# The split of transposed probabilities in two attention mixers, with and without the scheduler's priority

## The chip, the cores and the metric

The kernel runs on one core of a Trainium2 chip. The metric is the device time of one execution in microseconds (us); lower is better. Engines are named as in the profile: PE is TensorE, with PEld for its weight loads, DVE is VectorE, ACT is ScalarE, POOL is GpSimd and SP is SyncE.

## What is computed

Two layers of a bidirectional encoder run over 768 tokens (a prompt of 512 and a sample of 256) with a model width of 1024. Each layer is a half feed-forward block, a mixer, and a second half feed-forward block. The mixer of layer 0 joins a chunked spatial gating with a windowed attention with sinks; that of layer 1 is a neighbourhood attention on a grid.

```python
def even_layer(x, ...):
    x = x + 0.5 * swiglu(rmsnorm(x, f1_n), f1_g, f1_u, f1_d)
    x = x + mixer_ab(rmsnorm(x, mix_n), w_in, sgu_ln_g, sgu_ln_b, sgu_w, sgu_b, sink, w_out)
    x = x + 0.5 * swiglu(rmsnorm(x, f2_n), f2_g, f2_u, f2_d)

def mixer_ab(h, ...):
    z = h @ w_in
    zs = gelu(z[..., :1024]); u, vh = zs[..., :512], layer_norm(zs[..., 512:])
    vmix = einsum('gij,bnjgc->bnigc', sgu_w, vh) + sgu_b      # chunks of 128 tokens, 4 groups
    a_out = u * vmix
    b_out = window_gqa(rope_partial(q), rope_partial(k), v, sink)   # 8 heads, 2 of keys and values
    return concatenate([a_out, b_out]) @ w_out

def window_gqa(q, k, v, sink):
    s = (q @ k^T over blocks n-1, n, n+1 of 128 tokens) * 64 ** -0.5, masked to |distance| <= 128
    p = softmax(concatenate([s, sink]))[..., :-1]
    return p @ v

def mixer_c(h, w_qkv, rpb, w_out):
    q, k, v = h @ w_qkv                                        # 16 heads of 64
    return neighbourhood_attn(q, k, v, rpb) @ w_out            # window 8 x 16 on a grid 64 wide, with bias
```

## The kernel before

Activations lie channel-major: 1024 channels are eight tiles of 128 partitions, and the 768 tokens lie along the free axis in groups of 512 and 256. A product in fp32 is made of three products of halves: every operand is split into a high part, a cast made on ACT (L122 for weights, whi; L208 for data), and a low part, which DVE subtracts (L123, wlo; L209, with the names tl, vhl, ol and others). Weights come in blocks of 512 KB through SP's queue. PSUM is held in two pools, `mm` for projections (ps_mm) and `aux` for the rest (ps_aux), with four banks of 128x512 each; the next tile of a pool waits for the last reader of the bank that it takes over.

The order of PE's instructions is written by hand: generators are started with delays on a planned time, and each product lets those whose time has come emit theirs. The context around the whole build (L1767) fixes that order for PE alone. On the other engines a list scheduler places the instructions, each when its operands are expected and by a priority that follows the order in the code; `tc.high_priority()` lets what is emitted inside it go ahead of other ready work on its engine. It stands in a few places already, such as the norms.

Mixer 0 runs from about 545 to 715 us of the span. Its attention goes through 12 pairs of a key head and a block of queries. `score` makes the scores of four heads into aux banks, and `finish_rows` the softmax in place: maximum (L1097), its negative (L1101), four exponentials on ACT (L1103), the sink's part (L1107 to L1109), the reciprocal (L1111) and four scalings p (L1113). `turn` (L1222 on) transposes up to three blocks of p by PE into an aux bank each (L156) and splits each bank into th and tl, of which there are three buffers. `values` multiplies both by the values and adds the two halves of the result, through a copy tb on ACT (L1242) and additions on DVE (L1248).

Beside it run the projections of the queries, with their rotation (`roped`, L1153 to L1156: a shuffle ru and a product rt from the projection's bank, a product on ru, the sum), and then the high and low part of q (L1374). `stats` gets the gating input's mean and scale (mv, up to L1304), ACT applies them (L1310, vg), the split follows (vhh on ACT, vhl on DVE), PE mixes them with the gating weights (swh, swl), and L1319 adds the bias into the output tiles o. `u_part` projects the other half (L1350), applies the gelu on ACT (L1351) and multiplies it in (L1354).

Mixer 1 runs from about 1755 to 2065 us. Its attention works on pairs of heads; `split_t` (L1458 on) transposes four blocks of probabilities into one aux bank and splits it into th and tl. Beside it run the projections of q, k and v (qk at L1577, vt at L1594).

Of the kernel before, what the change touches and what calls it, by code (L numbers as in the profile page):

```python
# [55 lines left out]
class Trunk:  # L56
# [1061 lines left out]
    def mixer0(self):  # L1118
# [104 lines left out]
        def turn(kv, n, blks, p):  # L1223
            res = []
            for i, b in enumerate(blks):
                pt = self.psum(self.aux, "aux")
                for r in range(4):
                    self.tpose(pt[:, r * P : (r + 1) * P], p[r][:, i * P : (i + 1) * P])
                th = mp.tile([P, 512], F32R, tag="th", name="th", bufs=3)
                tl = mp.tile([P, 512], F32R, tag="tl", name="tl", bufs=3)  # L1230
                self.split(th, tl, pt)
                res.append((th, tl))
            return res

# [21 lines left out]
        def attention(gap):  # L1256
            cur = None
            for kv in (0, 1):
                for n in range(6):
                    while len(qheads) < 2 * kv + 2:  # L1260
                        yield 0.5
                    new = score(kv, qheads[2 * kv : 2 * kv + 2], n)
                    scored.append((kv, n))
                    yield gap
                    if cur:
                        values(*cur[:3], tt)
                        valued.append(cur[:2])
                    yield gap
                    cur = new
                    tt = turn(*cur)  # L1270
                    yield 0.3 * gap
            yield 1.0
            values(*cur[:3], tt)
# [125 lines left out]
    def mixer1(self):  # L1399
# [57 lines left out]
        def split_t(src):  # L1457
            pt = self.psum(self.aux, "aux")  # L1458
            for i, s in enumerate(src):
                self.tpose(pt[:, i * P : (i + 1) * P], s)  # L1460
            th = mp.tile([P, 512], F32R, tag="th", name="th", bufs=3)
            tl = mp.tile([P, 512], F32R, tag="tl", name="tl", bufs=3)
            self.split(th, tl, pt)
            return th, tl

        def put(h, po, c0, c1):
# [32 lines left out]
        def prompt(pr, p, vt, hv):  # L1499

            while len(vt) < 6:
                yield 0.5
            for h in (0, 1):
                a, b, c, d = p[0][h] + p[1][h]
                tt = []
                for src in ((a[:, lo], d[:, hi], a[:, hi], b[:, lo]), (b[:, hi], c[:, lo], c[:, hi], d[:, lo])):
                    tt.append(split_t(src))
                    yield GAPS1[1]
                yield GAPS1[2]
                po = self.psum(self.aux, "aux")  # L1510
                values_a(po, vt, hv + h, 0, tt[0])
                yield GAPS1[3]
                values_a(po, vt, hv + h, 1, tt[1])
                put(2 * pr + h, po, 0, TA)
                yield GAPS1[3]

        def sample(pr, p, vt, hv):
            tt = []
            for h in (0, 1):
                a, b = p[2][h]  # L1520
                tt.append(split_t((a[:, lo], b[:, lo], a[:, hi], b[:, hi])))
                yield GAPS1[1]
            yield GAPS1[2]
            for h in (0, 1):
                po = self.psum(self.aux, "aux")
                values_b(po, vt, hv + h, tt[h])
                put(2 * pr + h, po, TA, T)
                yield GAPS1[3]
# [291 lines left out]
```

## Time and profile before

| | |
|---|---|
| median of three runs | 2595.67 us (2592.29 to 2597.21) |
| the profiled execution | 2597.41 us |
| its span on the core | 2595.6 us |
| mean granted clock of PE | 0.994 |
| instructions | 41312 |

The span is what the profiler saw between the first and the last instruction; the execution's own time lies 1.8 us above it. Times of rows below count from the start of the span. A row of the timeline gives the start and the duration in us, the engine, the line of the kernel, the operation, output and inputs with the buffer numbers left out, their shapes, the number of merged instructions, and in brackets how long the engine had been idle before and what ended that wait. Neighbouring instructions of an engine overlap a little in such rows. A row of windows gives the busy time of each engine in a stretch, then the clock that PE was granted (PEclk, 1.00 is full speed).

### The profile page before, as it was taken

Reading aid. Unit: us, or ns where it says so; the run is one execution under the profiler, and the core shown is the slowest. Engines: PE = TensorE matmul, PEld = TensorE weight load, DVE = VectorE, ACT = ScalarE, POOL = GpSimd, SP = SyncE. Lnnn points to the kernel's source line nnn. Section 1 sums busy time; section 2 is a strip of 40 time slices with the busy share of each in tenths; the row PEclk is TensorE's granted clock in tenths of the full one; section 3 lists DMA queues with packets and bytes.
Section 4 is the critical chain, followed back from the end, with each engine's and each line's share of the span. In section 5 each row is a group of like instructions: output and inputs, shape, how many; then the busy total and the mean of one; then the engine's idle time right before and its main releaser. Section 6 shows DMA issues by size and latency. Waiting matters only on the chain.

```text
span 2595.6 us, 41312 instructions
## 1 busy us (share of the span) xinstructions
PE 2556.4 (98%) x15114; PEld 2491.2 (96%) x15114; DVE 2232.9 (86%) x4659; ACT 1365.6 (53%) x2869; POOL 159.7 (6%) x255
## 2 busy tenths in 40 slices
PE   8999999999999999999999999999999999999998
PEld 8899999988899999999999999998998999999997
DVE  7898889888789998889998888986676699888897
ACT  7454454556656544445655445454454565444543
POOL 1000000000022000000100000002222220000000
PEclk9999999999999999999999999999999999999999
DMA  7523222321135322223442222142221344222222
GB/s 253 160 84 111 66 74 74 130 93 45 49 111 165 103 66 66 77 70 98 125 120 74 73 66 82 66 142 66 64 64 41 106 130 123 82 71 77 70 68 75
DMA packets 93372, 238.68 MB, mean 92 GB/s; under 512 B 21488, under 2 KB 34288, under 8 KB 93168
## 3 DMA queue, kind: packets, MB, share of 16 engines
q1 hardware_dynamic: 85712, 218.96, 26.5%
q0 software_dynamic: 7168, 16.78, 3.0%
q8 instruction: 119, 1.95, 0.3%
q14 instruction: 85, 0.70, 0.1%
q10 hardware_dynamic: 288, 0.29, 0.0%
HBM read 226.56 MB, written 15.07 MB: 93 GB/s over the span
## 4 chain that ended last, share of the span: by engine, by line
PE 68%; DVE 4%; ACT 1%; issue 1%; DMA 0%; DVEq 0%; ACTq 0%
PE ps_mm L152 41%; PE ps_aux L152 25%; PE ps_aux L156 1%; DVE wlo L123 0%; DVE tmp L415 0%; ACT p L1103 0%; DVE p L1113 0%; DVE p L1097 0%; DMA raw<-in_w 0%; ACT whi L122 0%; DVE tl L209 0%; DVE qk L1577 0%; DVE sg L589 0%; ACT diag L306 0%; DVE v L588 0%
## 5 line engine op out<-in xcount | busy, mean ns | idle before, releaser
L122 ACT CAST whi<-s 128x512 fp32r<-128x512 f32 x496 | 304.6, 620 | 404.5 <-DVE s L737 179.2
L122 ACT CAST whi<-raw 128x512 fp32r<-128x512 f32 x504 | 306.1, 619 | 224.3 <-PE ps_mm L152 95.3
L123 DVE TENSOR_TENSOR wlo<-s,whi 128x512 fp32r<-128x512 f32 x496 | 336.6, 684 | 59.9 <-ACT whi L122 50.4
L123 DVE TENSOR_TENSOR wlo<-raw,whi 128x512 fp32r<-128x512 f32 x468 | 319.9, 692 | 17.4 <-ACT whi L122 14.2
L152 PE MATMUL ps_aux<-dt,whi 128*128 128x384 f32 x864 | 221.8, 337 | 5.1 <-ACT whi L122 5.1
L152 PE MATMUL ps_mm<-db,whi 128*128 128x384 f32 x864 | 219.3, 334 | 0.0
L152 PEld LDWEIGHTS ps_aux<-dt,whi 128*128 128x128 f32 x864 | 157.7, 190 | 5.8 <-ACT whi L122 5.8
L152 PEld LDWEIGHTS ps_mm<-db,whi 128*128 128x128 f32 x864 | 156.0, 188 | 0.0
L152 PE MATMUL ps_aux<-dt,wlo 128*128 128x384 f32 x432 | 145.7, 337 | 0.2 <-DVE wlo L123 0.2
L152 PE MATMUL ps_mm<-xh,whi 128*128 128x512 f32 (+1 forms) x416 | 145.7, 350 | 0.0
L152 PE MATMUL ps_mm<-db,wlo 128*128 128x384 f32 x432 | 144.3, 334 | 0.0
L152 PE MATMUL ps_mm<-xh,wlo 128*128 128x512 f32 (+1 forms) x416 | 140.8, 338 | 0.0
L152 PE MATMUL ps_mm<-xl,whi 128*128 128x512 f32 (+1 forms) x416 | 140.8, 338 | 0.0
L737 DVE TENSOR_TENSOR s<-raw,raw 128x512 f32<-128x512 f32 x124 | 83.9, 685 | 25.1 <-DMA raw<-in_w 25.0
L577 DVE TENSOR_TENSOR u<-ps_aux,u 128x384 f32<-128x384 f32 x176 | 96.9, 551 | 7.6 <-PE ps_aux L152 7.4
L793 DVE TENSOR_TENSOR x<-ps_aux,x 128x384 f32<-128x384 f32 x160 | 85.3, 551 | 15.6 <-PE ps_aux L152 15.6
L152 PE MATMUL ps_aux<-dh,whi 128*128 128x384 f32 x384 | 97.5, 334 | 0.0
L123 POOL TENSOR_TENSOR wlo<-raw,whi 128x512 fp32r<-128x512 f32 x36 | 48.5, 1355 | 746.0 <-ACT whi L122 738.1
L1103 ACT ACTIVATE p<-p,st 128x256 f32<-128x256 f32 (+3 forms) x144 | 69.0, 480 | 47.9 <-DVE st L1101 47.8
L793 DVE TENSOR_TENSOR x<-ps_mm,x 128x384 f32<-128x384 f32 x160 | 85.8, 550 | 5.8 <-PE ps_mm L152 5.5
L572 ACT COPY u<-ps_mm 128x384 f32<-128x384 f32 x176 | 83.4, 474 | 10.7 <-PE ps_mm L152 10.4
L152 PEld LDWEIGHTS ps_mm<-xh,whi 128*128 128x128 f32 x416 | 79.2, 190 | 9.1 <-issue 0.8
(516 smaller groups left out, 8143.1 us busy)
## 6 DMA issues: line engine op xcount, KB each, us to landing
raw<-in_w SPq DMA_DIRECT2D x346, 512.0 KB, 3.7
s<-in_w POOLq DMA_DIRECT2D x64, 256.0 KB, 4.9
xdm<-x SPq DMA_DIRECT2D x16, 384.0 KB, 2.4
x<-in_x SPq DMA_DIRECT2D x16, 192.0 KB, 5.4
tok<-in_xt SPq DMA_DIRECT2D x12, 256.0 KB, 6.9
xold<-xdm SPq DMA_DIRECT2D x8, 384.0 KB, 3.1
x<-xdm SPq DMA_DIRECT2D x8, 384.0 KB, 4.5
out_y<-y SPq DMA_DIRECT2D x8, 384.0 KB, 2.6
```

Of the source, the lines that this page charges most:

```text
L122: nc.scalar.copy(hi, src)
L123: (eng or nc.gpsimd).tensor_tensor(out=lo, in0=src, in1=hi.bitcast(F32), op=ALU.subtract)
L152: self.nc.tensor.matmul(out, lhsT=lhsT, rhs=rhs, start=start, stop=stop, **kw)
L156: self.nc.tensor.transpose(out, src, self.ident)
L572: nc.scalar.copy(e[n, out], bank[key, n])
L577: nc.vector.tensor_tensor(out=t, in0=bank[key, n], in1=t, op=ALU.add)
L737: f = lambda o, x, y, op: self.nc.vector.tensor_tensor(out=o, in0=x, in1=y, op=op)
L793: nc.vector.tensor_tensor(out=o, in0=ps, in1=o, op=ALU.add)
L1103: ins = nc.scalar.activation(outs[i], outs[i], AF.Exp, bias=nm[:, i : i + 1], accum_out=sm[:, i : i + 1])
```

## The change

In `turn` of mixer 0 and in `split_t` of mixer 1 the split of a transposed block, that is the copy to th on ACT and the subtraction to tl on DVE, stands inside `tc.high_priority()`.

```diff
@@ -1228,7 +1228,8 @@
                 th = mp.tile([P, 512], F32R, tag="th", name="th", bufs=3)
                 tl = mp.tile([P, 512], F32R, tag="tl", name="tl", bufs=3)
-                self.split(th, tl, pt)
+                with self.tc.high_priority():
+                    self.split(th, tl, pt)
                 res.append((th, tl))
@@ -1460,7 +1461,8 @@
             th = mp.tile([P, 512], F32R, tag="th", name="th", bufs=3)
             tl = mp.tile([P, 512], F32R, tag="tl", name="tl", bufs=3)
-            self.split(th, tl, pt)
+            with self.tc.high_priority():
+                self.split(th, tl, pt)
             return th, tl
```

No instruction is added or removed. The orders of PE, POOL and SP are the same before and after. On DVE and ACT the order differs at some 26 places, all in the two mixers. Lines behind the first edit are one higher after the change (L1248 is L1249), those behind the second two.

The first place is on ACT, about 585 to 592 us, in mixer 0, where the casts of two blocks of the gating input (vhh), a weight's cast (whi452), the copy tb of an attention result, and the exponentials of the next softmax (p) meet. Before:

```order
L208 CAST vhh_6498<-vg_6339 128x512
L208 CAST vhh_6582<-vg_6341 128x512
L122 CAST whi452_6608<-raw104_6602 128x512
L1242 COPY tb_6389<-ps_aux435_6384 64x512
L1103 ACT_TABLE_LOAD
L1103 ACTIVATE p_6476,st_6480<-p_6476,st_6480 128x384
L1103 ACTIVATE p_6477,st_6480<-p_6477,st_6480 128x384
```

After the change:

```order
L208 CAST vhh_6498<-vg_6339 128x512
L1103 ACT_TABLE_LOAD
L1103 ACTIVATE p_6476,st_6480<-p_6476,st_6480 128x384
L1243 COPY tb_6389<-ps_aux435_6384 64x512
L1103 ACTIVATE p_6477,st_6480<-p_6477,st_6480 128x384
L1103 ACTIVATE p_6478,st_6480<-p_6478,st_6480 128x384
L1103 ACTIVATE p_6479,st_6480<-p_6479,st_6480 128x384
L1108 ACTIVATE st_6480<-st_6480 128x4
L208 CAST vhh_6582<-vg_6341 128x512
L122 CAST whi452_6608<-raw104_6602 128x512
```

The table load and one exponential now stand ahead of tb, and the second vhh and the weight's cast behind all exponentials.

The second place is on DVE at the same time: the low parts vhl of the gating input, small steps of the softmax (st), a weight's low part (wlo452), the additions that read tb, and the rotation of a query projection whose bank is ps_mm434. Before:

```order
L209 TENSOR_TENSOR vhl_6499<-vg_6339,vhh_6498 128x512
L1101 TENSOR_SCALAR st_6480<-st_6480 128x4
L209 TENSOR_TENSOR vhl_6583<-vg_6341,vhh_6582 128x512
L1107 TENSOR_TENSOR st_6480<-sink_5702,st_6480 128x4
L123 TENSOR_TENSOR wlo452_6609<-raw104_6602,whi452_6608 128x512
L1248 TENSOR_TENSOR o4_5934<-ps_aux435_6384,tb_6389 64x128 x2
L1248 TENSOR_TENSOR o5_5935<-ps_aux435_6384,tb_6389 64x128 x2
L1153 STREAM_SHUFFLE ru_6447<-ps_mm434_6380 128x512
L1154 TENSOR_TENSOR rt_6446<-ps_mm434_6380,rct_5694 128x512
```

After the change:

```order
L209 TENSOR_TENSOR vhl_6499<-vg_6339,vhh_6498 128x512
L1249 TENSOR_TENSOR o4_5934<-ps_aux435_6384,tb_6389 64x128 x2
L1249 TENSOR_TENSOR o5_5935<-ps_aux435_6384,tb_6389 64x128 x2
L1153 STREAM_SHUFFLE ru_6447<-ps_mm434_6380 128x512
L1155 TENSOR_TENSOR ru_6447<-ru_6447,rst_5695 128x512
L1109 TENSOR_TENSOR st_6480<-st_6480 128x4
L209 TENSOR_TENSOR vhl_6583<-vg_6341,vhh_6582 128x512
L1111 RECIPROCAL st_6480<-st_6480 128x4
L123 TENSOR_TENSOR wlo452_6609<-raw104_6602,whi452_6608 128x512
L1154 TENSOR_TENSOR rt_6446<-ps_mm434_6380,rct_5694 128x512
```

The additions come right behind the first vhl, and the product rt, the last to read ps_mm434, comes behind the second vhl and the weight's low part.

The third place is on DVE, about 630 to 636 us, still in mixer 0: the additions of one result, the rotation of another query projection, and two low parts tl. Before:

```order
L1248 TENSOR_TENSOR o5_5935<-ps_aux472_6916,tb_6921 64x128 x2
L1153 STREAM_SHUFFLE ru_6931<-ps_mm471_6891 128x512
L1154 TENSOR_TENSOR rt_6930<-ps_mm471_6891,rct_5694 128x512
L1155 TENSOR_TENSOR ru_6931<-ru_6931,rst_5695 128x512
L209 TENSOR_TENSOR tl_7002<-ps_aux477_6996,th_7001 128x512
L1156 TENSOR_TENSOR rt_6930<-rt_6930,ru_6931 128x512
L209 TENSOR_TENSOR tl_7011<-ps_aux478_7005,th_7010 128x512
```

After the change:

```order
L1249 TENSOR_TENSOR o5_5935<-ps_aux472_6916,tb_6921 64x128
L209 TENSOR_TENSOR tl_7002<-ps_aux477_6996,th_7001 128x512
L209 TENSOR_TENSOR tl_7011<-ps_aux478_7005,th_7010 128x512
L1249 TENSOR_TENSOR o5_5935<-ps_aux472_6916,tb_6921 64x128
L1153 STREAM_SHUFFLE ru_6931<-ps_mm471_6891 128x512
L1154 TENSOR_TENSOR rt_6930<-ps_mm471_6891,rct_5694 128x512
L1155 TENSOR_TENSOR ru_6931<-ru_6931,rst_5695 128x512
```

Both tl stand ahead of the rotation, and of the last addition.

## The prediction

> **What bounds the kernel now.** I read the page's busy times, then TensorE's waits, then the two stretches in which the mixers run.
>
> ```profile
> PE 2556.4 (98%) x15114; PEld 2491.2 (96%) x15114; DVE 2232.9 (86%) x4659; ACT 1365.6 (53%) x2869; POOL 159.7 (6%) x255
> ```
>
> TensorE (PE) works for 98% of the span; nothing else comes near. The change adds and removes no instruction and leaves PE's order as it was, so it can only shorten or lengthen PE's waits, or change the clock that PE is granted. Among the waits of PE, grouped by what ended them (total us, times, longest), the one on the low parts that the split makes:
>
> ```profile
> PE ps_aux L152 <- DVE tl L209: 4.4, 7, 1.5
> ```
>
> **The change aims at this row, 4.4 us in seven waits.** That is 0.17% of the time and the most that its own purpose can return, clock aside. The stretches of the two mixers (length, then busy us of PE, PEld, DVE, ACT, POOL; PEclk, DMA share, GB/s):
>
> ```profile
> 545.00:715.00 170.00, 161.13 (x927) 137.25 (x926) 139.02 (x410) 103.18 (x225) 7.32 (x5) 0.96 0.17 55
> 1755.00:2065.00 310.00, 306.79 (x2213) 281.64 (x2212) 215.35 (x627) 156.82 (x412) 70.09 (x148) 1.00 0.22 67
> ```
>
> Mixer 0 leaves PE idle for 8.9 of 170 us, mixer 1 for 3.2 of 310. In mixer 0 VectorE (DVE) is busy for 82%, so a job that goes ahead pushes another back, and each place must be followed to the next thing that PE needs from DVE.
>
> **Place A, near 580 to 606 us: a loss.** Before the change ScalarE (ACT) and DVE go like this:
>
> ```profile
> 584.88 1.12 ACT L208 CAST vhh<-vg 128x512 fp32r<-128x512 f32 x2
> 585.91 0.61 ACT L122 CAST whi<-raw 128x512 fp32r<-128x512 f32 x1
> 586.55 0.58 ACT L1242 COPY tb<-ps_aux 64x512 f32<-64x512 f32 x1
> 587.15 1.28 ACT L1103 ACT_TABLE_LOAD   x1
> 588.45 0.62 ACT L1103 ACTIVATE p<-p,st 128x384 f32<-128x384 f32 x1
> ```
> ```profile
> 586.20 0.69 DVE L209 TENSOR_TENSOR vhl<-vg,vhh 128x512 fp32r<-128x512 f32 x1
> 586.80 0.16 DVE L1107 TENSOR_TENSOR st<-sink,st 128x4 f32<-128x4 f32 x1
> 586.87 0.69 DVE L123 TENSOR_TENSOR wlo<-raw,whi 128x512 fp32r<-128x512 f32 x1
> 587.47 1.17 DVE L1248 TENSOR_TENSOR o<-ps_aux,tb 64x128 f32<-64x128 f32 x4
> ...
> 588.68 0.74 DVE L1153 STREAM_SHUFFLE ru<-ps_mm 128x512 f32<-128x512 f32 x1
> 589.32 0.67 DVE L1154 TENSOR_TENSOR rt<-ps_mm,rct 128x512 f32<-128x512 f32 x1
> ```
> ```profile
> 590.68 0.45 PE L152 MATMUL ps_mm<-whi,xh 128*128 128x512 f32 x1
> ...
> 596.94 0.66 PE L156 MATMUL ps_aux<-ident,p 128*128 128x128 f32 x4 [1.66 <-DVE o L1319]
> 598.11 0.30 PE L152 MATMUL ps_aux<-swh,vhh 128*128 128x128 f32 x1 [0.52 <-DVE o L1248]
> ...
> 601.59 0.73 PE L152 MATMUL ps_mm<-whi,xh 128*128 128x512 f32 x1
> ```
>
> Two split blocks go ahead of the statistics of the gating input, whose chain (L1304, L1310, cast) then starts about one DVE instruction of 0.7 us later, so that the first vhh cast ends near 586.2 (585.5 before). Behind it ACT now takes the table load (1.28) and the first exponential (0.62), and only then the tb copy (0.58): 586.2 + 1.28 + 0.62 + 0.58, less the small overlaps of neighbours, is 588.8. DVE stands in order before L1248, which needs tb: it starts at 588.8 for 587.47, and DVE idles since the two jobs that stood there (second vhl, wlo) now stand behind it.
>
> Next comes the rope product L1154, the last reader of the bank of PSUM that the projection at 590.68 will write. It was the second after L1248; now L1155, L1109, the second vhl, L1111 and the wlo stand before it. Neighbours on DVE overlap by some 0.08, as the starts in these rows show, so a 128x512 job takes 0.6 and a 128x4 one 0.1: 0.6 + 0.1 + 0.7 (the vhl waits a little for its cast) + 0.1 + 0.6 = 2.1 us. Before, it ended at 589.99, ahead of PE's need. Now: 588.8 + 1.1 (L1248) + 0.7 (shuffle) + 2.1 + 0.67 = **593.4**. PE arrives about 590.8, so a new wait of 2.6 us appears there. It is not the whole loss, and not all loss, since PE waited later anyway, at 596.94 and 598.11. The projection takes 3.5 us (590.68 to 594.20) and eight transposes 0.97, so PE is at the third block's transposes at 593.4 + 4.5 = 597.9. These need the tl before them, which DVE, late by now, gives at about 598.9 (start of before 596.94); the mixed gating block behind them starts at 599.5 (598.11), and its third product needs a vhl that stands behind a tl, two L1248 and an L1319, at about 602.5. The next projection starts near 603.7.
>
> To compare, what the clock did in before must come off:
>
> ```profile
> 596.55:599.96 3.41, 2.50 (x21) 2.29 (x21) 3.34 (x10) 1.65 (x4) 0.00 (x0) 1.00 0.00 0
> 599.96:606.79 6.83, 6.83 (x30) 5.47 (x29) 5.50 (x19) 0.42 (x1) 0.00 (x0) 0.50 0.23 77
> 637.50:640.91 3.41, 3.41 (x10) 2.62 (x9) 3.41 (x16) 0.51 (x3) 0.00 (x0) 0.50 0.00 0
> ```
>
> From 599.96 on PE ran at 0.50, and the 1.63 us up to 601.59 lost somewhat under half, some 0.7, to that; at full clock they would have ended at 600.9. **A is 603.7 − 600.9 = +2.8.** Bounds: +1.4 if only the late L1248 counts, −2.2 if both old waits (1.66 + 0.52) go and no new one comes, +4.3 if the last part runs at half clock. I take +2.8, which is what the rows give when followed one by one.
>
> **Place B, near 628 to 650: nothing.** Both tl here go ahead of an L1248 and of a rope.
>
> ```profile
> 635.48 0.33 PE L152 MATMUL ps_aux<-swh,vhh 128*128 128x128 f32 x1 [1.46 <-DVE tl L209]
> ```
> ```profile
> 633.00:648.00 15.00, 13.54 (x92) 12.15 (x92) 14.71 (x48) 8.06 (x19) 0.00 (x0) 0.89 0.05 16
> ```
> ```profile
> 646.12 2.16 DVE L1319 SCALAR_TENSOR_TENSOR o<-ps_aux,lng,sb 128x128 f32<-128x128 f32 x8
> ```
> ```profile
> 648.35 0.39 PE L152 MATMUL ps_aux<-kh,q 64*128 64x256 f32 x2
> ```
>
> The 1.46 us wait goes: the gating block can start about 634.2. But DVE is busy for 14.71 of the 15 us up to 648, with the same instructions in another order, and ends its L1319 at 648.28 as before. The scores at 648.35 write a bank that this L1319 reads last, so they can't start earlier: PE, ahead by 1.3, waits at the gating's vhl, at L1248's o and in the end here. What is late next is this L1319. Worth 0; bounds: 0 and −(1.46 + 1.6), where 1.6 is the half clock of the window 637.50 to 640.91 (about half of 3.41 us), which followed that wait.
>
> **C to F, small.**
>
> ```profile
> 661.99 1.03 DVE L1354 TENSOR_TENSOR o<-o,ug 128x512 f32<-128x512 f32 x2 [1.10 <-ACT ug L1351]
> ```
> ```profile
> 663.67 0.44 PE L152 MATMUL ps_aux<-kh,q 64*128 64x384 f32 x1 [0.91 <-DVE tl L209]
> ```
> ```profile
> 1831.75 0.94 DVE L1113 TENSOR_SCALAR p<-p,st 128x160 f32<-128x160 f32 x4
> ```
> ```profile
> 1832.44 0.28 PE L152 MATMUL ps_aux<-th,vt 128*128 128x256 f32 x1
> 1833.35 0.39 PE L152 MATMUL ps_aux<-tl,vt 128*128 128x256 f32 x1 [0.62 <-DVE tl L209]
> 1833.57 0.28 PE L152 MATMUL ps_aux<-th,vt 128*128 128x256 f32 x1
> 1833.69 0.28 PE L152 MATMUL ps_aux<-tl,vt 128*128 128x256 f32 x1
> ```
> ```profile
> 1974.43 0.48 DVE L1594 SCALAR_TENSOR_TENSOR vt<-ps_mm,sm,vt 128x256 fp32r<-128x256 f32 x1
> ```
> ```profile
> 1975.56 0.39 PE L152 MATMUL ps_aux<-tl,vt 128*128 128x256 f32 x1 [0.42 <-DVE tl L209]
> ```
> ```profile
> 2010.66 0.42 DVE L1577 TENSOR_TENSOR qk<-ps_mm,rt 128x256 f32<-128x256 f32 x1
> ```
> ```profile
> 2011.80 0.44 PE L152 MATMUL ps_mm<-ol,whi 128*128 128x384 f32 x1 [0.92 <-DVE ol L209]
> ```
>
> C: the tl pass the second of two L1354, worth at most half of its 1.03, 0.5; I take **−0.3**, since the tl can't start before its th. D, in mixer 1: the tl pass L1111 and four L1113, which took 0.9. The product followed its neighbour by 0.91 instead of the 0.12 of the next pair, so 0.79 is all there is: **−0.8**. E: the tl passes one L1594 (0.40 from start to start), out of a lateness of 0.42: **−0.4**. F: the ol waited for here falls behind one more qk of 0.33: **+0.3**. The other moves of mixer 1 push probabilities (L1113) back by 1 to 3 us; their transposes come 11 us or more later, and DVE is busy for only 69% there. Worth 0, since PE idles for just 3.2 us in the whole of mixer 1; without that cover one such move costs its tl's 0.7.
>
> Sum: 2.8 + 0 − 0.3 − 0.8 − 0.4 + 0.3 = **+1.6**. The profiled execution took 2597.41, with a span of 2595.6; 2599.0 by its own time. The median of the three runs is 2595.67, 1.74 below it, so on the median the forecast is **2597.3**. The clock is taken to be as it was, two half windows near A; bounds −3.4 (they go) to +3.4 (two more, each 1.7).
>
> **The rivals.** First, the wait of place B really goes, with the half clock behind it: 2597.3 − 3.06 = 2594.2. For it: the largest single wait for tl in mixer 0. Against it: DVE is full to 648.28. It needs the L1319 to come earlier than it did, which no row supports. Only with A at its lower end besides (−2.2 for +2.8) does the time go below 2590.5. Chance 0.17, of which 0.06 lies below 2590.5.
>
> Second, the other side: the new stall of 2.6 us at 590.8 makes PE lose its clock. In the rows above the window 596.55 to 599.96, with 0.91 us of PE idle inside and 1.66 partly ahead of it, is followed by 6.83 us, two such windows, at 0.50, and the wait of 1.46 at 635 by one. A stall of 2.6 is longer than either. If it costs one window more, or two, that is +1.7 or +3.4, and with A's last part at half clock (+4.3 for +2.8) the time is 2597.3 + 1.7 + 1.5 = 2600.5 up to 2602.2. It decides at the window's place: if the stall is cut by a window's border into two halves, neither may count, and part of the lost clock only replaces the windows at 599.96. Chance 0.20, of which 0.15 lies above 2600.9. The Trainium skill, "TensorE: Matmul & The Clock Gate", section "HAM oscillation — how this bites in real kernels", gives as a rule "no PE-idle gaps >~3.4µs". By it a stall of 2.6 us leaves the clock alone, and the forecast stands with no second rival. The trace differs: 0.50 after single gaps of 1.66 and 1.46 us, so the rival keeps its chance.
>
> Third, everything is covered: the late L1154 and the late tl eat only what PE would have waited anyway, and A is 0. Then −1.2 is left, 2594.5. For it: DVE's total is unchanged, and PE waited 2.2 us in A before. Against it: the rows put L1154 2.6 us behind PE's arrival. Chance 0.18.
>
> **How the numbers follow.** Forecast 0.45, the first rival 0.17, the second 0.20, the third 0.18. About 0.2%, 5.2 us, is what a measurement of this kernel can tell from no change: faster is below 2590.5, slower above 2600.9. Faster 0.06, slower 0.15, same 0.79. The range reaches from 2591.0 (near the first rival with part of A gained) to 2602.3 (two windows more).
>
> **What would show it.** Right: a wait of some 2.6 us of PE on the rope product (rt, L1154 of before) near 591; DVE idle before L1248 near 587; no wait for tl at 635, and instead small waits on vhl, o and the scores' bank up to 650; no waits for tl at 1833 and 1975; PE's order unchanged. Wrong: no wait near 591 (A is covered), the scores of 648.35 earlier by over 1 us against the work before them (B is real), or half windows near 594 (the clock).

## The result and the profile after

The median of 19 runs is 2599.13 us (2595.17 to 2601.83), against 2594.39 us of before (19 runs, 2591.77 to 2598.29). The ratio is 1.0018 with a 95% interval of 1.0012 to 1.0024, that is +4.7 us, between 3.1 and 6.2: slower, but by less than the 0.2% at which the prediction drew its line. The profiled execution took 2600.40 us with a span of 2598.6.

The page of after, busy time of the engines. PE's instructions and their order are the same; its busy time grew by 0.9 us of the 3.0 us by which the span grew, the rest is waiting.

```profile
PE 2557.3 (98%) x15114; PEld 2490.6 (96%) x15114; DVE 2238.2 (86%) x4659; ACT 1365.2 (53%) x2869; POOL 159.6 (6%) x255
```

The waits of PE after (total us, times, longest):

```profile
PE ps_mm L152 <- DVE wlo L123: 6.0, 7, 1.8
PE ps_aux L152 <- ACT whi L122: 5.1, 2, 4.4
PE ps_mm L152 <- DVE ol L209: 2.9, 2, 2.0
PE ps_mm L152 <- DVE rt L1154: 2.7, 1, 2.7
...
PE ps_aux L152 <- DVE vhl L209: 2.1, 2, 1.1
...
PE ps_aux L152 <- DVE tl L209: 1.2, 4, 0.6
PE ps_aux L156 <- DVE tl L209: 1.0, 1, 1.0
```

The row that the change aims at fell from 4.4 us in seven waits to 1.2 in four. In its place stand a wait of 2.7 on the rope product (rt), 2.1 on vhl, 2.9 instead of 1.8 on ol, and one of 1.0 of the transposes (L156), which wait for a tl before them. At place A, VectorE, ScalarE and PE after:

```profile
584.08 0.69 DVE L209 TENSOR_TENSOR vhl<-vg,vhh 128x512 fp32r<-128x512 f32 x1 [0.66 <-ACT vhh L208]
586.71 1.17 DVE L1249 TENSOR_TENSOR o<-ps_aux,tb 64x128 f32<-64x128 f32 x4 [1.94 <-ACT tb L1243]
```
```profile
583.44 0.60 ACT L208 CAST vhh<-vg 128x512 fp32r<-128x512 f32 x1
584.06 1.28 ACT L1103 ACT_TABLE_LOAD   x1
585.36 0.62 ACT L1103 ACTIVATE p<-p,st 128x384 f32<-128x384 f32 x1
585.88 0.19 ACT L1103 ACTIVATION_READ_ACCUMULATOR p<-p,st 128x1 f32 x1
586.09 0.58 ACT L1243 COPY tb<-ps_aux 64x512 f32<-64x512 f32 x1
```
```profile
591.41 0.79 PE L152 MATMUL ps_mm<-whi,xh 128*128 128x512 f32 x1 [2.69 <-DVE rt L1154]
599.71 0.66 PE L156 MATMUL ps_aux<-ident,p 128*128 128x128 f32 x4 [0.96 <-DVE tl L209]
603.29 0.33 PE L152 MATMUL ps_aux<-swh,vhl 128*128 128x128 f32 x1 [1.01 <-DVE vhl L209]
```

This execution came to the place 2.1 us earlier than that of before. The reader sees the table load and an exponential between vhh and tb, VectorE idle for 1.94 us before the additions, and three waits of PE where before stood two. At place B the wait for tl at 635 is gone, and this one is new:

```profile
644.69 0.33 PE L152 MATMUL ps_aux<-swh,vhl 128*128 128x128 f32 x1 [1.08 <-DVE vhl L209]
```

The windows of PE's clock in the mixers after, and the one before the first of them (length, busy us of PE, PEld, DVE, ACT, POOL; PEclk):

```profile
587.13:590.54 3.41, 1.59 (x14) 1.41 (x12) 3.29 (x10) 3.41 (x11) 0.00 (x0) 1.00 0.00 0
590.54:597.37 6.83, 5.96 (x14) 4.70 (x15) 5.58 (x16) 1.69 (x4) 0.00 (x0) 0.50 0.29 79
604.19:607.60 3.41, 3.41 (x19) 2.62 (x18) 2.92 (x8) 0.00 (x0) 0.00 (x0) 0.50 0.22 53
645.15:648.56 3.41, 3.41 (x18) 3.41 (x18) 3.12 (x13) 2.74 (x6) 0.00 (x0) 0.50 0.00 0
2013.90:2017.31 3.41, 3.41 (x15) 3.31 (x15) 2.43 (x6) 1.93 (x6) 0.00 (x0) 0.50 0.19 23
```

Half clock begins in the last part of the wait on rt (590.54 and on) and follows those on vhl (604.19, 645.15) and on ol (2013.90).

To part waits from clock I compare, in both profiles, the time between the same two instructions of PE, and take off half of PE's busy time in windows at 0.50 (what full speed would have saved). The result is the cost at equal clock:

| stretch in the trace of before, us | forecast | after | clock lost before, after |
|---|---|---|---|
| A, 579 to 608 | +2.8 | +2.9 | 3.4, 4.7 |
| B, 625 to 655 | 0 | +0.5 | 1.7, 1.7 |
| C, 655 to 690 | -0.3 | -0.6 | 0, 0 |
| end of mixer 0, 690 to 760 | 0 | 0.0 | 1.7, 0 |
| D, 1755 to 1900 | -0.8 | -1.1 | 0, 0 |
| E, 1900 to 1990 | -0.4 | -0.5 | 0, 0 |
| F, 1990 to 2065 | +0.3 | +1.3 | 0, 1.7 |
| sum | +1.6 | +2.5 | 6.8, 8.1 |

Outside these stretches, where the edit changes nothing, the two profiles differ by another +1.0 at equal clock, between 760 and 1755 us above all; this is taken as chance: the ten other profiles without added waits lie between -1.6 and -0.2 there. One profile has chance in its windows too (+1.3 for the clock here), so the clock term is better read from all runs: the granted clock was 0.9937 on average in the 19 runs of after, 0.9947 in the 82 runs of before beside the first ten experiments. 0.0010 of 2595 us is 2.5 us, with a 95% interval of 1.5 to 3.6. Waits of +2.5 and a clock of +2.5 make +5.0 against the measured 4.7.

At F the cause of the extra loss stands in the trace. The scalings on VectorE and the next subtraction on GpSimd before:

```profile
2008.61 0.95 DVE L1113 TENSOR_SCALAR p<-p,st 128x160 f32<-128x160 f32 x4
```
```profile
2010.05 1.28 POOL L123 TENSOR_TENSOR wlo<-raw,whi 128x512 fp32r<-128x512 f32 x1 [3.06 <-ACT whi L122]
```

VectorE and GpSimd after:

```profile
2009.60 1.98 DVE L1113 TENSOR_SCALAR p<-p,st 128x160 f32<-128x160 f32 x4
2011.50 0.41 DVE L1375 SCALAR_TENSOR_TENSOR ql<-qk,qh 128x256 fp32r<-128x256 f32 x1
2011.84 1.01 DVE L209 TENSOR_TENSOR ol<-o,oh 128x384 fp32r<-128x384 f32 x2
```
```profile
2009.57 1.28 POOL L123 TENSOR_TENSOR wlo<-raw,whi 128x512 fp32r<-128x512 f32 x1 [3.05 <-ACT whi L122]
```
```profile
2012.43 0.44 PE L152 MATMUL ps_mm<-ol,whi 128*128 128x384 f32 x1 [2.04 <-DVE ol L209]
```

Four scalings took 1.98 us where the same four took 0.95 before (at 2008.61, when GpSimd was idle until 2010.05). They now start 0.03 us behind a subtraction on GpSimd; the first of them ended 0.1 us after it. PE's wait for ol grew from 0.92 to 2.04.

### The profile page after: what moved, and what is told of

Read it like the earlier page. It is cut to its first block, busy times and chain, and to the rows that moved or that the text cites. A ratio compares the mean times of both kernels' runs of the same rounds, so it can differ in the third digit from the quotient of the medians.

```text
span 2598.6 us, 41303 instructions
## 1 busy us (share of the span) xinstructions
PE 2557.3 (98%) x15114; PEld 2490.6 (96%) x15114; DVE 2238.2 (86%) x4659; ACT 1365.2 (53%) x2869; POOL 159.6 (6%) x255
## 3 DMA queue, kind: packets, MB, share of 16 engines
q8 instruction: 119, 1.95, 0.3%
## 4 chain that ended last, share of the span: by engine, by line
PE 67%; DVE 4%; ACT 1%; DMA 1%; issue 0%; DVEq 0%; SPq 0%; ACTq 0%
PE ps_mm L152 41%; PE ps_aux L152 25%; PE ps_aux L156 1%; DMA raw<-in_w 1%; DVE wlo L123 0%; DVE tmp L415 0%; DVE p L1113 0%; ACT p L1103 0%; ACT whi L122 0%; DVE acc L235 0%; DVE ol L209 0%; DVE p L1097 0%; DMA mf<-in_nmask 0%; DVE tmp L393 0%; DVE tl L209 0%
## 5 line engine op out<-in xcount | busy, mean ns | idle before, releaser
L737 DVE TENSOR_TENSOR s<-s,raw 128x512 f32<-128x512 f32 x124 | 85.2, 687 | 4.5 <-DMA raw<-in_w 3.7
```

The source lines that it names most:

```text
L737: f = lambda o, x, y, op: self.nc.vector.tensor_tensor(out=o, in0=x, in1=y, op=op)
```

## The experiments

Each kernel was timed beside the kernel before, in 4 to 11 runs. In the diffs a condition stands in place of the plain priority.

**Which part loses: four parts alone.** One mixer alone is the change with one of its two edits undone. One turn alone, and mixer 0 without it (`!=` in place of `==`), both leave mixer 1 as before:

```diff
-                with self.tc.high_priority():
+                with self.tc.high_priority() if (kv, n) == (0, 1) else nullcontext():
                     self.split(th, tl, pt)
```

> Priority in mixer 0 alone (mixer 1 as before). Place-by-place theory: a wait of 2.6 to 2.8 us of TensorE on the rope product near 591, half clock behind it, the late tl and vhl after it; stretch 579 to 607 us longer by about 4.4 us, place B 0, place C -0.5: +3.5 to +4.5 us, ratio 1.0014 to 1.0017. Rival, mixer 1 carries the loss: under +1.5 us (1.0006). Rival, the difference has nothing to do with single places (every build with the edit is slower by about the same): +4.7 us.

Measured: 2598.26 us, ratio 1.0017 (1.0008 to 1.0026), wait on rt 2.68 us, A +2.9 at equal clock.

> Priority in mixer 1 alone (mixer 0 as before). Place-by-place theory: the waits near 1833 and 1975 us go (-0.8, -0.5), the wait for ol near 2012 us grows from 0.9 to 2.0 us, and a window of half clock may follow it (+1.7): -0.3 to +1.5 us in all, ratio 0.9999 to 1.0006. Rival, mixer 1 carries the loss: +3 us or more (1.0012). Rival of no single place: +4.7 us.

Measured: 2594.50 us, 1.0001 (0.9992 to 1.0009). The waits at 1833 and 1975 are gone (D -0.9, E -0.5), that for ol is 2.01, with half clock behind it (F +1.1).

> Priority in one call of turn alone, that of key head 0 and query block 1, which the orders show to be the one that moves ScalarE and VectorE at 579 to 607 us; the 11 others and mixer 1 as before. Place-by-place theory: the wait of 2.7 us on the rope product is there, and nearly all of the loss of mixer 0: +4 to +4.9 us, ratio 1.0015 to 1.0019, and the wait of 1.46 us for tl at 635 is back. Rival, TensorE makes up for the late rope product later, since it waited there anyway: under +1 us (1.0004). Rival of no single place: between 0 and +4.7, without the wait.

Measured: 2597.66 us, 1.0014 (1.0005 to 1.0023). In its profile a half window at 582.75, ahead of the place, slowed PE, so that the wait on rt was only 1.25 and one of 1.41 on the additions (o) followed; A +1.1 at equal clock. The wait expected at 2.7 was thus missed, and the time, 1.0014, lies just below the 1.0015 to 1.0019 that were expected. This profile does not show where the time goes: by the clock on the wall its stretch A is 0.6 us shorter than that of before, which lost more to half clock. That this turn loses is read from the times.

> Priority in mixer 0 in all calls of turn but that of key head 0 and query block 1; mixer 1 as before. Place-by-place theory: no wait on the rope product; the wait of 1.46 us for tl at 635 is gone, but TensorE waits again for vhl near 644, so place B stays at 0 within 0.5, place C -0.5: -1 to 0 us, ratio 0.9996 to 1.0000. If the wait at 635 really is worth its length and the half clock behind it: -3 us (0.9988). Rival of no single place: +4 us or so.

Measured: 2593.97 us, 0.9999 (0.9991 to 1.0008). No wait on rt; the wait of 1.46 at 635 is gone, but vhl is waited for 1.08 us at 641 with a half window right behind (B +0.4), C -0.5. A is +0.8 in this profile, and between +0.1 and +0.8 in all five profiles in which that turn has no priority; a number of this kind can't be read more finely.

What follows: the loss is in mixer 0, and there in one of twelve calls of `turn`. Mixer 1 gives and takes. The rivals that put it in mixer 1, or nowhere in particular, are out, and so is the thought that PE makes the stall good later.

**What in place A loses.** By the orders the one turn does two things: its two tl push the gating input's statistics back by 0.7 us, and then the table load and the exponentials overtake tb and the second vhh on ScalarE. The rope product writes a buffer of a tag with three (L1123) that the gating inputs vg, rt, ru and tb share, and it stands behind the vhl that frees one (a fourth buffer was not tried: it moves much else). The first kernel undoes the second vhh's fall, the second keeps the exponentials behind tb.

```diff
-            self.split(*vs, v)
+            with self.tc.high_priority() if n == 1 else nullcontext():
+                self.split(*vs, v)
```
```diff
-            nc.scalar.copy(tb, po[64:128, :])
+            copies.append(nc.scalar.copy(tb, po[64:128, :]).ins)
...
+            with self.tc.issue_after(after) if after is not None else nullcontext():
                 ins = nc.scalar.activation(
                     outs[i], outs[i], AF.Exp, bias=nm[:, i : i + 1], accum_out=sm[:, i : i + 1]
...
+                after=copies[0] if (kv, n) == (0, 2) else None,
```

> Priority in the one turn of key head 0 and query block 1, as in the run of that turn alone, and besides for the split (vhh, vhl) of the gating input of token block 1. By the orders this puts that vhh back ahead of the table load and vhl ahead of the additions that read tb, so that the rope product no longer stands behind vhl and a weight's low part; the table load and one exponential stay ahead of tb. Buffer theory: the rope product came late since its output takes the buffer that vhl frees, and vhl came late since its cast went behind the exponentials; its wait on TensorE falls from 2.7 to about 1 us, and the stretch 579 to 608 us loses about 1 us at equal clock instead of 2.9: ratio 1.0003 to 1.0008. Rival, the late tb (behind table load and exponential) alone makes the wait: it stays at 2.5 us or grows by the 0.5 us of the cast: ratio 1.0014 or more.

Measured: 2598.98 us, 1.0016 (1.0008 to 1.0025). The wait on rt fell to 1.07 as the buffer theory said, but the time did not fall: PE's waits in its profile are

```profile
590.42 0.50 PE L152 MATMUL ps_mm<-whi,xh 128*128 128x512 f32 x1 [1.07 <-DVE rt L1154]
596.19 0.66 PE L156 MATMUL ps_aux<-ident,p 128*128 128x128 f32 x4 [1.20 <-DVE o L1321]
598.36 0.44 PE L152 MATMUL ps_aux<-swh,vhh 128*128 128x128 f32 x1 [1.51 <-DVE o L1249]
```

with three half windows from 598.08 on; A is +1.6 at equal clock, not about 1, and the ratio is the one of the rival, though the wait is not.

> Priority in the one turn of key head 0 and query block 1, as in the run of that turn alone; besides, the exponentials of the next softmax (query block 2) are issued after the copy tb. By the orders ScalarE then stands as before the change (vhh, vhh, the weight's cast, tb, table load, exponentials), and VectorE keeps only the two tl ahead of the gating input's statistics. Theory, the loss comes from the table load and the exponentials overtaking tb and the second vhh: no idle time of 1.9 us of VectorE before the additions, the wait on the rope product falls from 2.7 to at most 0.4 us, the stretch 579 to 608 us costs 0 to 0.8 us at equal clock instead of 2.9: ratio 0.9999 to 1.0006. Rival, the loss comes from the statistics that the two tl push back by 0.7 us: the wait stays above 1.5 us, ratio 1.0012 or more.

Measured: 2598.00 us, 1.0015 (1.0006 to 1.0024). The wait on rt is gone, and VectorE has no idle time before the additions; A is +1.2 at equal clock, not 0 to 0.8, and the ratio missed its range; it lies in that of the rival, whose wait did not come. PE waits here:

```profile
597.61 0.66 PE L156 MATMUL ps_aux<-ident,p 128*128 128x128 f32 x4 [1.27 <-DVE o L1323]
599.73 0.30 PE L152 MATMUL ps_aux<-swh,vhh 128*128 128x128 f32 x1 [1.45 <-DVE o L1252]
```

and VectorE, which is busy from 591 to 603 us:

```profile
597.48 0.68 DVE L209 TENSOR_TENSOR vhl<-vg,vhh 128x512 fp32r<-128x512 f32 x1
598.08 0.42 DVE L1378 SCALAR_TENSOR_TENSOR q<-rt,q 128x256 fp32r<-128x256 f32 x1
598.41 1.17 DVE L1252 TENSOR_TENSOR o<-ps_aux,tb 64x128 f32<-64x128 f32 x4
```

In before the additions stand ahead of that vhl:

```profile
596.80 1.17 DVE L1248 TENSOR_TENSOR o<-ps_aux,tb 64x128 f32<-64x128 f32 x4
598.00 0.69 DVE L209 TENSOR_TENSOR vhl<-vg,vhh 128x512 fp32r<-128x512 f32 x1
```

Here the vhl (0.6) is first. With 0.5 from the late statistics that is the 1.1 us by which the gating block starts later. So rt was the largest link and not the only one: VectorE is the bound of this stretch, and what the two tl displace comes out at the next wait. The rest of the 4 us is clock by the runs (0.9942 against 0.9950 in the runs of before beside them, some 2 us); the profile, with as many half windows at A as that of before, does not show it.

**What in place F loses.** In the first kernel mixer 1 alone keeps the priority, but not for pair 6 (`if pr != 6`); in the second, for all pairs, but GpSimd's subtraction goes to VectorE:

```diff
-            hi, lo = self.wsplit(loaded[4][:, :, c : c + P])
+            hi, lo = self.wsplit(loaded[4][:, :, c : c + P], nc.vector if name == "l1_w_out" and m == 0 else None)
```

> Priority in mixer 1 alone, in all calls but those of the seventh pair of heads (pair 6), whose th and tl go between the exponentials and ahead of the scalings near 2008 us. Place-by-place theory: the wait for ol near 2012 is back at 0.9 us and no half clock follows it, the waits near 1833 and 1975 stay away: -1.3 to -1.6 us against before, ratio 0.9994. Rival, that pair does not matter: as mixer 1 alone, ratio 1.0001.

Measured: 2593.43 us, 0.9996 (0.9987 to 1.0005). The wait for ol is 0.88, without a half window; D -0.8, E -0.5, F -0.3 instead of +1.1. The times of this kernel and of mixer 1 alone don't part (their intervals overlap); the traces do.

> Priority in mixer 1 alone, all calls; besides, the one low part of a weight that GpSimd computes at 2009.6 to 2010.8 us is computed by VectorE, where it stands 15 instructions after the scalings and behind all the ol. Shared-access theory: the first scaling (L1113, 128x160) took 1.35 us instead of 0.29 because it waited until GpSimd's instruction ended; it takes 0.29 here and the wait for ol falls from 2.0 to about 1.0 us, the clock window after it may go too: ratio 0.9993 to 0.9998. Rival, the scaling was slow for another reason (the first after a product that reads PSUM, or the semaphore): it stays at 1.3 us and the wait at 2.0 us, ratio 1.0001.

Measured: 2601.79 us, 1.0031 (1.0018 to 1.0043), far off what was expected, but for a reason of its own. The four scalings and PE's waits:

```profile
2002.99 0.93 DVE L1113 TENSOR_SCALAR p<-p,st 128x160 f32<-128x160 f32 x4
```
```profile
2004.78 0.45 PE L152 MATMUL ps_mm<-ol,whi 128*128 128x384 f32 x1 [0.93 <-DVE ol L209]
2013.39 0.69 PE L152 MATMUL ps_mm<-oh,wlo 128*128 128x384 f32 x1 [8.16 <-DVE wlo L123]
```

The disputed question is answered: without GpSimd beside them the scalings take 0.93, and the wait for ol is 0.93. The traces of all runs agree: of 448 such scalings (128x160) two ran beside a subtraction of GpSimd, in after and in mixer 1 alone, and took 1.35; none of the others took over 0.31. But the moved low part came behind all the ol, and PE needed it right after the first: 8.16 us, which I had overlooked. A queue that a step is moved into has its own order.

**The parts put together.** Both mixers without the two places, and both mixers with the exponentials behind tb and without pair 6:

> Priority in both mixers but for the two places that lost: not in the turn of key head 0 and query block 1, and not in pair 6 of mixer 1. By the sum of the two parts measured or expected alone (-0.3 and -1.4): -1 to -2.5 us, ratio 0.9991 to 0.9997, the only version so far that would be faster than before. Rival, the small gains are lost to TensorE's clock: ratio 1.0000.

Measured: 2593.11 us, 0.9997 (0.9988 to 1.0006).

> The change in both mixers in all calls but pair 6 of mixer 1, with the exponentials of query block 2 issued after the copy tb. By the parts (0 to 0.8 for that place, B 0.4, C -0.5, the rest of mixer 0 as it was, mixer 1 without pair 6 -1.4): -1.5 to +0.3 us, ratio 0.9994 to 1.0001, against 1.0018 of the change. Rival, the loss of the change lies elsewhere too: 1.0008 or more.

Measured: 2592.86 us, 0.9999 (0.9990 to 1.0009). Both take the loss of the change back (1.0018); neither is shown to be faster than before. In the profile of the second A is +1.5 at equal clock, with one half window instead of two: its waits end at 595.08 and 598.99, 3.9 us apart, where those of the run with that fix alone end 2.1 us apart. By the count in the last section this spares a window: its first window with a wait (from 593.11) stays just above the border of 3050 columns with 3062, its second (596.52) falls to 1896; in the run with that fix alone two windows in a row, 1646 and 2096, lie below it.

**What a wait costs in clock, by itself.** Into the kernel before, at places where PE never waited, such waits were put:

```diff
+        if self.pi in STALLS:
+            self.nc.tensor.transpose(ps[:, :P], self.zeros[:, :P], self.ident)
+            for _ in range(18):
+                self.nc.gpsimd.memset(self.zeros, 0.0)
+            self.nc.tensor.transpose(ps[:, :P], self.zeros[:, :P], self.ident)
```

> The kernel before, with ten waits of TensorE added in the feed-forward blocks between 870 and 1640 us, 70 us or more apart, where TensorE had no idle time: a transpose of a tile of zeros, 18 memsets of that tile on GpSimd that wait for it, and a second transpose that waits for the memsets; each wait is meant to be about 2.7 us, like the new one on the rope product. Clock theory: each is followed by one or two windows of 3.41 us at a granted clock of 0.50, so each costs its length and 1.7 to 3.4 us more: 44 to 61 us in all for waits of 2.7 us. Rival, waits shorter than 3.4 us leave the clock alone: the time grows by the length of the waits, 27 us, and no window at 0.50 follows them.

Measured: 2668.91 us, 1.0282 (1.0268 to 1.0296). The waits came out longer than meant. Its waits of PE on the zeros, and the windows about one of them:

```profile
PE ps_aux L151 <- POOL zeros L150: 33.9, 7, 4.8
PE ps_mm L151 <- POOL zeros L150: 14.5, 3, 4.8
```
```profile
954.32:957.73 3.41, 0.00 (x0) 0.00 (x0) 2.55 (x5) 0.73 (x2) 2.66 (x14) 1.00 0.63 163
957.73:961.14 3.41, 2.99 (x10) 2.99 (x11) 0.48 (x1) 0.00 (x0) 0.31 (x2) 0.50 0.50 149
961.14:964.55 3.41, 3.41 (x22) 3.41 (x21) 3.29 (x7) 1.20 (x3) 0.00 (x0) 1.00 0.00 0
```

All ten waits of 4.8 us were followed by half clock, eight by 6.83 us of it and two by 3.41. The time rose by 73 us (0.0282 x 2595): 48.4 us of waits, 22 us for half of PE's 44.2 busy us in those half windows, and the rest for the added transposes.

> The same with 35 waits made by three memsets, meant to be about 0.7 us each, 16 us or more apart, in the same blocks. Clock theory: such a wait is too short to halve the clock, so the time grows by the sum of the waits alone, about 25 us, hardly a window at 0.50. Rival, any wait costs clock: windows at 0.50 behind most of them, 60 us or more in all.

Measured: 2641.84 us, 1.0180 (1.0167 to 1.0194). The added zeros change part of the output here, and where they do so was not traced; PE has the 70 transposes more and its other work as before. The waits and the stretch:

```profile
PE ps_aux L151 <- POOL zeros L150: 18.1, 20, 0.9
PE ps_mm L151 <- POOL zeros L150: 13.6, 15, 0.9
```
```profile
870.00:1740.00 870.00, 838.61 (x4817) 827.86 (x4816) 747.39 (x1388) 425.05 (x844) 32.48 (x118) 1.00 0.25 78
```

35 waits of 0.91 us, not one followed by half clock. The time rose by 47 us, 31.7 of them waits; the rest, 15 us, is 0.2 us for each of 70 added transposes, whose rows last 0.27 to 0.33 and overlap with neighbours. So short waits cost their length and long ones more; the length in between, 1 to 3 us, which is that of the mixers' waits, was meant to be tested and was not.

## Why the prediction was right, and where not

- **Range and side held.** 2597.3 was forecast, 1.6 us over before, in 2591.0 to 2602.3; measured +4.7. "Within 0.2%" got the largest chance and is what came, near its edge. The forecast change is a third of the measured one, and the range would have held no change as well. That 2597.3 lies within 1.8 us of 2599.13 is in part luck: the median of before was 2595.67 in the three runs known then and is 2594.39 in 19.
- **A was right in mechanism and in size.** A wait of 2.6 us on rt was forecast, 2.69 came (and 2.68 in mixer 0 alone); moved by the 2.1 us that this execution was early, the additions start at 588.8 and rt ends at 593.5 (forecast 588.8 and 593.4); the tl and the vhl behind it were late as worked out; +2.8 against +2.9 at equal clock. The sum for tb gives 588.68 as written, not 588.8; it leaves out the read of the exponential's accumulator, 0.19 us, that stands before tb. The buffer that ties rt to the second vhl was not seen, only its trace in the order.
- **B was right.** The wait at 635 went and PE gave its lead back at vhl (1.08 us at 644.69), and half clock with it: +0.5 for 0. The first rival fell in each run that had the priority there. Its 1.6 us for the half clock were hardly there to gain: in the run of one turn alone the wait at 635 is there (1.51) and no half window follows, yet the stretch takes 0.3 us longer than in before.
- **C, D and E** were right in sign and a little small: -0.3, -0.8, -0.4 forecast, -0.6, -1.1, -0.5 found.
- **F was mis-sized.** "The ol waited for here falls behind one more qk of 0.33" gave +0.3; it was +1.3 at equal clock. The scalings moved too, onto GpSimd's subtraction, and the first of them waited for it. The exponentials also ended later, since both th went between them. I had followed the order on VectorE alone, not what runs beside a moved instruction.
- **The clock term is the step that failed.** "The clock is taken to be as it was, two half windows near A" put it at 0; it measured about +2.5, half of the loss. The second rival had the size (+1.7 to +3.4) and a chance of 0.20, but not all of the place: in the two profiles A loses 1.3 us more to half clock, F 1.7 more, the end of mixer 0 1.7 less. Where waits of over 1 us are made, the expected clock belongs into the sum and not into the range alone.
- The third rival, that all is covered, fell with the wait on rt. The rule of the Trainium skill, "TensorE: Matmul & The Clock Gate", section "HAM oscillation — how this bites in real kernels" (no gap above some 3.4 us), agrees with the pair of added waits, 4.8 and 0.9 us; it does not hold for the mixers, where waits of 1.1 to 2.7 us were followed by half clock.

## What to carry to other kernels

A priority for the step that the bound engine waits for pushes back other work on the engine that does it. Here the waits aimed at went at little cost where VectorE was busy for 69% of the time (D and E), and came back elsewhere where it was busy for 82% (A and B); follow the displaced work to the next bank, buffer or vhl that is waited for, and to what runs beside it on other engines (F). Judge each call by itself: one of twelve calls made nearly all the loss here. Count a wait of TensorE at its length, and look at how much work it leaves to the clock window around it.

## What the runs showed of the hardware that was not expected

- **Which waits halve the clock.** In the 14 profiles, outside the added waits and leaving out the program's first 140 and last 100 us, 52 waits of PE lasted 0.8 to 1.0 us; within 3.5 us of 3 of them half clock began. Of 30 waits of 1.0 to 1.6 us it did so behind 20, of 8 of 1.6 to 1.75, all in place A, behind 6; of 14 of 1.75 to 1.95, all at the end of mixer 0, behind 2; of 5 of 2 to 3 us behind 4. Length alone doesn't decide: the same wait is followed by it in one run and not in the next.
- **The work in a fixed window parts them.** In each profile all changes of the clock lie whole multiples of 3.41 us apart, so the same parts of the 14 profiles can be cut into such windows. Count for each window the columns that PE's products stream (512 for 128*128 128x512), a product on 64 of the 128 rows for half and a transpose double. A window at full clock has 7560 in the median. Of 64 windows with fewer than 3050, all are followed by half clock; of 9625 with more, one is (3132). Windows that are themselves at half clock follow the same border. With transposes counted once, 65 of 79 windows below 3050 are followed by it, and none of those above. In before the window from 596.55 has 3012 and the one from 593.13 4632; in after the wait on rt leaves 2052 to the window from 587.13. Of the 14 waits at the end of mixer 0 the two that half clock followed fell into windows of 2776 and 3012, the others left 3260 or more in each; the 35 short added waits left 3685 or more. So a wait of 1 to 2 us halves the clock where it falls into one window and the work around it is thin, and not where a border cuts it in two. The count was made after all runs, and the border and the double weight were fitted to these 14 profiles; no run tested them, and why transposes should count double is open.
- **A scaling on VectorE waited for a subtraction on GpSimd that had started just before it**: four scalings took 1.98 us beside GpSimd's 1.28, 0.93 and 0.95 without it, and the first ended just behind it. The Trainium skill, "SBUF — State Buffer", section "Who interferes with whom", says that such an instruction of VectorE and one of GpSimd share a port that the one that starts first holds to its end; the trace agrees.
